# Hybrid encoder block: exponentials kept in SBUF, eight score buffers, reciprocals by four, other PSUM banks, and w's high parts on GpSimd

## The chip, the cores and the metric

The kernel runs on one core of a Trainium2 chip. Its metric is the device time of one launch in microseconds. PE is TensorE's matrix multiplier, PEld its weight loads, DVE is VectorE, ACT is ScalarE, POOL is GpSimd and SP is SyncE, which here only issues DMAs.

## The reference

One mixer layer on x of 1024 tokens by 1024 features: one projection into eight column sections, two kinds of attention, a gate, an output projection, and a LayerNorm with a scaled residual. All in float32.

```python
h = jnp.einsum('bsd,de->bse', x, w_in[layer])
q_a, k_a, v_a, z_a, q_b, k_b, v_b, z_b = jnp.split(h, SPLIT_POINTS, axis=-1)
y_a = neighborhood_attention(q_a, k_a, v_a, rel_pos_bias[layer])    # 8 heads of 64; 16 x 64 grid, window 8 x 16
qb = rotary(q_b, positions)                                         # 8 query heads
kb = rotary(k_b, positions)                                         # 2 key and value heads
y_b = windowed_gqa_with_sink(qb, kb, v_b, sink_logits[layer])       # |i - j| <= 128, softmax with one sink logit more
mixed = jnp.concatenate([y_a * jax.nn.silu(z_a), y_b * jax.nn.silu(z_b)], axis=-1)
y = jnp.einsum('bse,ed->bsd', mixed, w_out[layer])
x = layer_norm(DEEPNORM_ALPHA * x + y, ln_gain[layer], ln_bias[layer])
```

## The kernel before

Every float32 factor of a matmul is split into a high and a low 16-bit part, and a product is three matmuls: high by high, high by low and low by high (`xf`, `wh`, `wl`, `split`, `m`, `wo` are such parts). There are three phases: a prologue (values, scales, the first six projections), the stage of the attention units with the other 15 projections filled in between, and the output projection with the LayerNorm (`final`).

The order of the first two phases is written out by hand: each engine runs its instructions in the order in which the program issues them, and waits at each for what it needs. The stage is a loop over steps `i`, one attention unit a step, 128 units: first group b (64 units, the grouped-query heads with the sink), then group a (64 units, the neighbourhood heads). A unit is 128 queries of one head against 256 or 384 keys. Four units make a quad. Names and lines:

- `stage_load` (L766) runs seven steps ahead of a unit and loads the bias of a head in group a.
- `stage_qk` (L778) multiplies queries and keys on PE into a PSUM bank `ps_s` (L800). Of these there are four, used in turn. Then one DVE instruction (L807) adds mask or bias, writes the negated scores to an SBUF buffer `sn` (four, in turn) and leaves the row minimum in `nm`. In group b the column after the scores holds the negated sink, which DVE copies there (L804) for the first four units of a head pair.
- `stage_exp` (L813) lets ACT write the exponentials back into the PSUM bank of the scores (L822), with their row sums in `sm`.
- `stage_ri` (L825) makes the reciprocals of two row sums on DVE (L827) and scales them by 2 to the 14 (L828), every second step, ahead of that step's `stage_qk`.
- `stage_tr` (L832), `LTT` = 2 steps after the scores, reads the exponentials in the PSUM bank twice: ACT writes the normalised high part (L838) and DVE the low part (L839) to a `split` tile, of which there are `NSPLIT` = 6. A DMA from SP transposes it into a `tr` tile, of which there are `BH` = 9. L839 is the last to read the score bank.
- `stage_pv` (L849) multiplies a quad's transposed tiles with the values on PE (L867), `LPP` + 3 = 9 steps after the quad's first scores. Two quads share one PSUM bank `ps_t`, of which there are two. `stage_gate` (L870) multiplies the sum with the gate on DVE (L878, L881).
- `project` (L362) makes one section of 128 columns in 48 groups of matmuls (L382) into the banks `ps_pj`, of which there are two. `new_group` (L357) sees to it that the evacuation of the group two before has been issued. `w_split` (L185) splits a half of a section's weights: ACT writes the high part (L193), POOL scales the raw weights (L198) and subtracts (L199).
- `FILL_AT` says at which steps the groups of each projection, and then of the first output matmuls (L1002), are put between the units on PE. The last five entries are those of the output matmuls.
- Work that no unit waits for stands in a queue for each engine (`enq`, L149), is taken from there a little at each step (`pop`, L161), and is issued at once where it is needed (`need`, L169).

## Time and profile before

| | us |
|---|---|
| median of 3 runs (472.32 to 1610.4) | 475.13 |
| the profiled execution | 474.88 |
| its span, first to last instruction | 473.2 |

A profile comes from one execution. A row of a group names the line, engine and operation, then output and inputs by the program's names with partitions x elements and type and the count; then the busy time in us and the mean of one in ns; then the idle time of the engine just before these instructions, in us, and what ended most of it. A row of the timeline has start and length in us, and in brackets the idle time before it and its releaser. Times of PE are modelled at their ends, so a busy PE need not be PE at its peak; idle time of PE is idle.

The slices of the page, 40 of 11.8 us each in tenths of busy time, show the three phases: prologue to slice 10, the units from slice 11 to 33, the output after that.

```
PE   8999999999988998998989998789897889999995
DVE  5969868169878899888987888788988875549955
ACT  5849689774689877776786877678786874602411
POOL 0200244748468359575332664455552304104731
```

### The profile page before, as it was taken

The numbers are of one execution on the slowest core, as the hardware profiler recorded it, in microseconds if no ns is written. First come the engines' busy times: TensorE is split into PE (matmuls) and PEld (weight loads), VectorE is DVE, ScalarE is ACT, GpSimd is POOL, SyncE is SP. The second block draws the span as 40 slices with busy tenths as digits, with TensorE's granted clock in tenths as the row PEclk, the third lists the DMA queues.
The fourth block names the chain that finished last, engine by engine and source line by source line (L and its number), as shares of the span: only waits on it lengthen the run. The fifth ranks groups of instructions, "written<-read, shape, count | busy, mean of one in ns | idle before, by whom it ended". The sixth has DMA issues, their size and how long they took to land. (4 is left out here: it accounts for less than half of the span.)

```text
span 473.2 us, 11261 instructions
## 1 busy us (share of the span) xinstructions
PE 440.9 (93%) x4214; PEld 283.9 (60%) x4214; DVE 372.0 (79%) x904; ACT 319.4 (68%) x700; POOL 208.5 (44%) x219
## 2 busy tenths in 40 slices
PE   8999999999988998998989998789897889999995
PEld 7997744444555766665766765556565565444444
DVE  5969868169878899888987888788988875549955
ACT  5849689774689877776786877678786874602411
POOL 0200244748468359575332664455552304104731
PEclk9999999999999999998999999999998999999999
DMA  8911779941298896685798486486587868501721
GB/s 275 388 57 47 245 219 317 308 157 43 79 194 164 171 175 131 109 144 111 142 142 121 82 158 124 74 139 125 107 161 141 145 113 273 202 0 66 224 89 68
DMA packets 123991, 71.33 MB, mean 151 GB/s; under 512 B 96800, under 2 KB 105888, under 8 KB 123936
## 3 DMA queue, kind: packets, MB, share of 16 engines
q1 hardware_dynamic: 123792, 70.48, 63.3%
q8 instruction: 33, 0.54, 0.5%
q14 instruction: 22, 0.18, 0.1%
q10 hardware_dynamic: 144, 0.13, 0.1%
HBM read 41.23 MB, written 6.29 MB: 100 GB/s over the span
## 5 line engine op out<-in xcount | busy, mean ns | idle before, releaser
L382 PE MATMUL ps_pj<-xf,wh 128*64 128x512 f16 (+1 forms) x1152 | 210.9, 381 | 0.0
L382 PE MATMUL ps_pj<-xf,wl 128*64 128x512 f16 (+1 forms) x576 | 134.3, 381 | 0.0
L382 PEld LDWEIGHTS <-wh 128*64 128x64 f16 (+1 forms) x1152 | 82.4, 108 | 47.1 <-issue 0.6
L839 DVE SCALAR_TENSOR_TENSOR split<-ps_s,ri,split 128x384 f16<-128x384 f32 (+1 forms) x128 | 74.6, 583 | 24.6 <-ACT split L838 22.2
L838 ACT ACTIVATE split<-ps_s,ri 128x384 f16<-128x384 f32 (+1 forms) x128 | 69.7, 545 | 31.8 <-issue 12.6
L822 ACT ACTIVATE ps_s<-sn,nm 128x385 f32<-128x385 f32 (+3 forms) x128 | 70.9, 554 | 20.3 <-DVE nm L807 19.2
L800 PE MATMUL ps_s<-ks,qs 128*64 128x384 f16 (+1 forms) x512 | 63.3, 318 | 21.9 <-DVE split L839 19.4
L1002 PEld LDWEIGHTS <-m 128*128 128x128 f16 (+1 forms) x492 | 42.6, 101 | 39.9 <-issue 1.4
L800 PEld LDWEIGHTS <-qs 128*64 128x64 f16 x512 | 33.8, 110 | 52.1 <-issue 31.2
L382 PEld LDWEIGHTS <-wl 128*64 128x64 f16 (+1 forms) x576 | 42.4, 109 | 28.1 <-issue 0.4
L198 POOL TENSOR_SCALAR wr<-wr,wsc 128x512 f32<-128x512 f32 x26 | 20.5, 789 | 74.3 <-ACT wh L193 63.5
L807 DVE CUSTOM_DVE_ANT_0 sn<-ps_s,bm,nsk 128x384 f32<-128x384 f32 (+1 forms) x64 | 40.7, 636 | 1.3 <-PE ps_s L800 1.0
L1002 PE MATMUL ps_s<-wo,m 128*128 128x512 f16 (+2 forms) x228 | 40.5, 368 | 0.4 <-DVE split L839 0.4
L807 DVE CUSTOM_DVE_ANT_0 sn<-ps_s,bias,sg 128x384 f32<-128x384 f32 (+1 forms) x64 | 37.0, 578 | 2.5 <-PE ps_s L800 1.0
L199 POOL TENSOR_TENSOR wl<-wr,wh 128x512 f16<-128x512 f32 x26 | 32.7, 1256 | 2.2
L299 POOL COPY ks<-ks 64x512 f16<-64x512 f16 x40 | 26.1, 660 | 8.5 <-ACT ks L251 3.9
L198 POOL TENSOR_SCALAR ws<-ws,wsc 128x512 f32<-128x512 f32 x16 | 11.1, 692 | 39.3 <-ACT wh L193 29.4
L828 DVE TENSOR_SCALAR ri<-ri 128x2 f32<-128x2 f32 x64 | 25.8, 403 | 2.2
L1057 ACT ACTIVATE sd<-mv,eps 128x1 f32<-128x1 f32 x8 | 2.4, 294 | 36.3 <-DVE mv L1055 34.9
L1101 POOL TENSOR_TENSOR xr<-xr,gb 128x512 f32<-128x512 f32 x7 | 9.8, 1396 | 38.4 <-ACT xr L1098 38.4
L1002 PE MATMUL ps_pj<-wo,m 128*128 128x512 f16 (+2 forms) x168 | 26.5, 333 | 0.0
L822 ACT ACTIVATION_READ_ACCUMULATOR ps_s<-sn,nm 128x1 f32 x128 | 24.2, 189 | 0.0
(184 smaller groups left out, 788.8 us busy)
## 6 DMA issues: line engine op xcount, KB each, us to landing
ws<-in_wt SPq DMA_DIRECT2D x15, 512.0 KB, 5.5
wr<-in_wt SPq DMA_DIRECT2D x26, 256.0 KB, 3.4
wor<-in_wo SPq DMA_DIRECT2D x22, 256.0 KB, 3.4
xr<-in_x SPq DMA_DIRECT2D x8, 512.0 KB, 9.4
out<-xr SPq DMA_DIRECT2D x15, 256.0 KB, 2.0
bias<-in_bias SPq DMA_DIRECT2D x8, 448.0 KB, 4.6
wvraw<-in_wv SPq DMA_DIRECT2D x9, 320.0 KB, 5.8
xraw<-in_xT SPq DMA_DIRECT2D x11, 256.0 KB, 5.1
```

What stands on the lines that cost most here:

```text
L198: nc.gpsimd.tensor_scalar(raw, raw, scale, 1.0, op0=ALU.mult, op1=ALU.mult)
L199: nc.gpsimd.tensor_sub(l, raw, h)
L299: nc.gpsimd.tensor_copy(place(t, o, half, col), place(t, a, half, col))
L382: nc.tensor.matmul(ps[c], a[:, k % 4, c], mv, start=(k == 0 and i == 0), stop=(k == KT - 1 and i == 2))
L800: nc.tensor.matmul(ps[c, :n], q[:, c], sl[i], start=(i == 0), stop=(i == 1))
L807: nc.vector.tensor_tensor_reduce(sn[:, :n], ps[:, :n], bias_t, sg[:, c:c + 1], init, op0=ALU.add, op1=ALU.min, accum_out=nm)
L822: nc.scalar.activation(pt[:, :m], sn[:, :m], AF.Exp, bias=nm, scale=-1.0, accum_out=sm[:, k % 2:k % 2 + 1])
L828: nc.vector.tensor_scalar_mul(ri, ri, PSCALE)
L838: nc.scalar.activation(hl[:, :m, 0, :], src, AF.Copy, scale=ri)
L839: nc.vector.scalar_tensor_tensor(hl[:, :m, 1, :], src, ri, hl[:, :m, 0, :], op0=ALU.mult, op1=ALU.subtract)
L1002: nc.tensor.matmul(ps[d, cs], lh[:, 128 * t + d.start:128 * t + d.stop], rh[:, cs], start=(e == EO[0] and i == 0), stop=(e == EO[-1] and i ...
L1101: nc.gpsimd.tensor_mul(xr[:, h1], xr[:, h1], gb[:, h1])
```

## The change

Nothing that is computed changes. The exponentials go into the score buffer in SBUF, one column to the left of the scores, so that the sink's column stays as it is. There are eight such buffers, and POOL writes the sinks into them seven steps ahead. The reciprocals are made for four units at a time, behind `stage_qk`, and the scaling becomes an instruction with two tensor inputs (its maximum with the unscaled value changes nothing). Splitting comes five steps after the scores, the values nine. There are five `split` tiles and eight `tr` tiles. Of the eight PSUM banks four stay for scores, one is left for values and three are for projections. For the projections of the unit stage POOL writes the high parts of w, too. In the prologue and in `final` the banks are named anew, and the last entries of `FILL_AT` move.

```diff
@@ -25,15 +25,15 @@
 PSCALE = 2.0 ** 14
 MSCALE = 2.0 ** -44
 QSCALE = 2.0 ** -15
-LTT, LPP, BH, ND, NA, NX, F1 = 2, 6, 9, 1, 1, 6, 0.2
-NSPLIT, NP = 6, 2
+LTT, LPP, BH, ND, NA, NX, F1 = 5, 9, 8, 1, 1, 6, 0.2
+NSPLIT, NSN, NP = 5, 8, 2
 ORDER = ["zb0", "z0", "zb1", "kb", "qb0", "z1", "qb1", "zb2", "qb2", "k0", "qb3", "zb3", "q0", "z2", "k1",
          "q1", "k2", "q2", "k3", "q3", "z3"]
 NPRO = 6
 NS = 21 - NPRO
 NR = 8
 FILL = ORDER[NPRO:]
-FILL_AT = [0, 8, 17, 25, 33, 41, 49, 57, 64.5, 71.5, 78, 85.5, 93, 101, 109, 121, 123.5, 126, 128, 131, 136]
+FILL_AT = [0, 8, 17, 25, 33, 41, 49, 57, 64.5, 71.5, 78, 85.5, 93, 101, 109, 121, 124, 127, 130, 133, 138]
 ZTAG = {"z3": "zv", "zb3": "zc", "z2": "zs", "zb1": "zd", "zb2": "ze"}
 KO = (2, 3, 4, 5, 6, 7, 0, 1)
 X1_AT = ((0,), (1,), (2,), (3, 4), (5,), (6, 7), (), ())
@@ -67,7 +67,7 @@
     ps1 = ctx.enter_context(tc.tile_pool(name="ps1", bufs=1, space=PS))
 
     def bank(tag):
-        bufs = {"pj": 2, "s": 4, "t": 2}[tag]
+        bufs = {"pj": 3, "s": 4, "t": 1}[tag]
         return (ps1 if bufs == 1 else ps2).tile([128, 512], F32, tag=tag, name=f"ps_{tag}", bufs=bufs)
 
     vd = dram.tile([4, GW, ROWS, 256], F16, name="vd")
@@ -198,11 +198,25 @@
             nc.gpsimd.tensor_scalar(raw, raw, scale, 1.0, op0=ALU.mult, op1=ALU.mult)
             nc.gpsimd.tensor_sub(l, raw, h)
 
+        def hi_pool():
+            h = wp.tile([128, 4, 128], F16, tag="wh", name=f"wh{m}", bufs=4)
+            l = wp.tile([128, 4, 128], F16, tag="wl", name=f"wl{m}", bufs=4)
+            parts[m] = (h, l)
+            nc.gpsimd.tensor_scalar(raws[m], raws[m], scale, 1.0, op0=ALU.mult, op1=ALU.mult)
+            nc.gpsimd.tensor_copy(h, raws[m])
+
+        def lo_pool():
+            nc.gpsimd.tensor_sub(parts[m][1], raws.pop(m), parts[m][0])
+
         g = min(m // 2, NPRO)
         scale = wsc[:, g:g + 1]
 
-        o = enq("act", hi, load_ops.get(("w", m)), prio=0.5)
-        o = enq("pool", lo, o, prio=0.5)
+        if g < NPRO:
+            o = enq("act", hi, load_ops.get(("w", m)), prio=0.5)
+            o = enq("pool", lo, o, prio=0.5)
+        else:
+            o = enq("pool", hi_pool, load_ops.get(("w", m)), prio=0.5)
+            o = enq("pool", lo_pool, o, prio=0.5)
         w_ops[m] = o
         if m + 5 < NL:
             load_ops["w", m + 5] = enq("sp", lambda: w_load(m + 5), o)
@@ -355,8 +369,8 @@
     groups = []
 
     def new_group():
-        if len(groups) >= 2:
-            need(*groups[-2])
+        if len(groups) >= 3:
+            need(*groups[-3])
         return bank("pj")
 
     def project(name):
@@ -567,7 +581,7 @@
         def v_max(t):
             nc.vector.tensor_reduce(vm[:, t:t + 1], v32[t], axis=AXX, op=ALU.max, apply_absolute_value=True)
 
-        tags = ("pj", "pj", "s", "s", "t", "t", "s", "s")
+        tags = ("pj", "pj", "s", "s", "t", "pj", "s", "s")
         banks = [bank(t) for t in tags]
         ordered.enter_context(tc.manual_schedule())
         first_tiles()
@@ -751,7 +765,7 @@
 
     units = unit_list()
     split = [ap.tile([128, 3, 2, 128], F16, name=f"split{i}", bufs=1) for i in range(NSPLIT)]
-    sns = [ap.tile([128, 388], F32, name=f"sn{i}", bufs=1) for i in range(4)]
+    sns = [ap.tile([128, 388], F32, name=f"sn{i}", bufs=1) for i in range(NSN)]
     for t in split:
         nc.gpsimd.memset(t, 0.0)
     LD = 7
@@ -765,6 +779,9 @@
 
     def stage_load(u, i):
         g, p, j, t = u
+        if g == "b" and t < NSN // 2:
+            h = 2 * p + j
+            nc.gpsimd.tensor_copy(sns[units.index(u) % NSN][:, 385:386], nsk[:, h:h + 1])
         if g == "a" and t == 0:
             bulk["last"] = clock["step"] + 1
             bt = big_ap([128, BWIN[3]], F32, "bias")
@@ -798,43 +815,38 @@
         for i in range(2):
             for c in HALVES:
                 nc.tensor.matmul(ps[c, :n], q[:, c], sl[i], start=(i == 0), stop=(i == 1))
-        s0 = sns[units.index(u) % 4]
-        sn = s0[:, 384 - n:]
-        if g == "b" and t < 2:
-            nc.vector.tensor_copy(s0[:, 384:385], nsk[:, h:h + 1])
+        sn = sns[units.index(u) % NSN][:, 385 - n:385]
         nm = ap.tile([128, 1], F32, tag="nm", name="nm", bufs=6)
         c = min(p, 1) if g == "b" else 2
-        nc.vector.tensor_tensor_reduce(sn[:, :n], ps[:, :n], bias_t, sg[:, c:c + 1], init,
+        nc.vector.tensor_tensor_reduce(sn, ps[:, :n], bias_t, sg[:, c:c + 1], init,
                                        op0=ALU.add, op1=ALU.min, accum_out=nm)
-        st[u, "sn"] = sn
-        st[u, "ps"] = ps
         st[u, "nm"] = nm
 
     def stage_exp(u):
-        n, _c = geom(u)
+        n, _m = geom(u)
         m = n + 1 if u[0] == "b" else n
-        sn, nm = st.pop((u, "sn")), st.pop((u, "nm"))
-        pt = st.pop((u, "ps"))
+        nm = st.pop((u, "nm"))
+        s0 = sns[units.index(u) % NSN]
         k = units.index(u) % 4
-        if k % 2 == 0:
-            st["sm"] = ap.tile([128, 2], F32, tag="sm", name="sm", bufs=4)
-        sm = st["sm"]
-        nc.scalar.activation(pt[:, :m], sn[:, :m], AF.Exp, bias=nm, scale=-1.0, accum_out=sm[:, k % 2:k % 2 + 1])
-        st[u, "p"] = pt
+        if k == 0:
+            st["sm"] = ap.tile([128, 4], F32, tag="sm", name="sm", bufs=4)
+        nc.scalar.activation(s0[:, 384 - n:384 - n + m], s0[:, 385 - n:385 - n + m], AF.Exp, bias=nm, scale=-1.0,
+                             accum_out=st["sm"][:, k:k + 1])
+        st[u, "p"] = s0[:, 384 - n:384]
 
     def stage_ri(i):
-        ri = ap.tile([128, 2], F32, tag="ri", name="ri", bufs=4)
+        ri = ap.tile([128, 4], F32, tag="ri", name="ri", bufs=4)
         nc.vector.reciprocal(ri, st["sm"])
-        nc.vector.tensor_scalar_mul(ri, ri, PSCALE)
-        for k in range(2):
-            st[units[i - 2 + k], "ri"] = ri[:, k:k + 1]
+        nc.vector.scalar_tensor_tensor(ri, ri, PSCALE, ri, op0=ALU.mult, op1=ALU.max)
+        for k in range(4):
+            st[units[i - 4 + k], "ri"] = ri[:, k:k + 1]
 
     def stage_tr(u):
         n, m = geom(u)
         ri = st.pop((u, "ri"))
         pt = st.pop((u, "p"))
         hl = split[units.index(u) % NSPLIT]
-        src = pt[:, :n].rearrange("p (k c) -> p k c", c=128)
+        src = pt.rearrange("p (k c) -> p k c", c=128)
         nc.scalar.activation(hl[:, :m, 0, :], src, AF.Copy, scale=ri)
         nc.vector.scalar_tensor_tensor(hl[:, :m, 1, :], src, ri, hl[:, :m, 0, :],
                                        op0=ALU.mult, op1=ALU.subtract)
@@ -1114,7 +1126,7 @@
                     normed[0] += 1
 
         halves, normed = {}, [0]
-        for t, tag in ((0, "t"), (1, "t"), (2, "s")):
+        for t, tag in ((0, "t"), (1, "s"), (2, "pj")):
             obank[t, 1] = bank(tag)
             list(out_mms(t, 1, obank[t, 1], EO[:4]))
         for e in EO[4:]:
@@ -1122,7 +1134,7 @@
                 list(out_mms(t, a, obank[t, a], [e]))
                 if e == EO[-1]:
                     finish(t, a, obank[t, a])
-        tags = iter(("pj", "t", "pj", "t", "s", "s", "s", "s"))
+        tags = iter(("pj", "t", "pj", "s", "pj", "s", "s"))
         for t, a in ((3, 1), (4, 1), (5, 0), (5, 1), (6, 0), (6, 1)):
             ps = bank(next(tags))
             list(out_mms(t, a, ps, EO))
@@ -1181,8 +1193,6 @@
             m_queue(4 + M_AT.index(i))
         if bulk["last"] != i or (queues["sp"] and i - queues["sp"][0].born > 2):
             pop("sp", 1 if i < 118 else 3)
-        if i % 2 == 0 and 2 <= i <= NU:
-            stage_ri(i)
         if i < NU:
             u = units[i]
             if u[0] == "b" and u[3] in (0, 4):
@@ -1190,6 +1200,8 @@
             if u[0] == "a" and u[3] == 0:
                 need(*stk_ops[u[1], u[2], 0], *stk_ops[u[1], u[2], 1])
             stage_qk(u)
+        if i % 4 == 0 and 4 <= i <= NU:
+            stage_ri(i)
         q, m = divmod(i - LP - 3, 4)
         if i >= Q30 + 2:
             q, m = (NU // 4 - 2, i - Q30 - 2) if i < Q30 + 4 else divmod(i - LP - 3, 4)
```

## The prediction

> **What bounds the kernel now.** I read the page first (engines, slices), then a table of two stretches, then the waits, then one stretch of the timeline.
>
> ```profile
> span 473.2 us, 11261 instructions
> PE 440.9 (93%) x4214; PEld 283.9 (60%) x4214; DVE 372.0 (79%) x904; ACT 319.4 (68%) x700; POOL 208.5 (44%) x219
> ```
>
> The one timed execution behind this page took 474.88 us: 1.7 us around the span of 473.2. That is 0.25 us under the median of the runs shown, so I make the sum against 474.9.
>
> The change touches the attention units, which run from about 125 to 389 us. The table has group b (130 to 250) and group a (250 to 390); its columns are busy us of PE, PEld, DVE, ACT and POOL, then the granted clock.
>
> ```profile
> 130.00:250.00 120.00, 109.37 (x1378) 75.98 (x1376) 104.69 (x292) 95.01 (x232) 70.91 (x71) 0.99 0.83 150
> 250.00:390.00 140.00, 125.73 (x1607) 86.07 (x1605) 116.47 (x304) 105.96 (x257) 63.05 (x75) 0.99 0.68 123
> sum 260.00, PE 235.11 PEld 162.05 DVE 221.16 ACT 200.96 POOL 133.96; mean PE 117.55 PEld 81.02 DVE 110.58 ACT 100.48 POOL 66.98
> ```
>
> PE is idle for 260.0 - 235.1 = 24.9 us here, DVE for 38.8. What they wait for (total us, times, longest):
>
> ```profile
> DVE split L839 <- ACT split L838: 22.2, 56, 1.5
> PE ps_s L800 <- DVE split L839: 19.4, 29, 2.4
> DVE ri L827 <- ACT ps_s L822: 6.3, 21, 0.8
> ACT split L838 <- ACT wh L193: 4.5, 6, 1.0
> ```
>
> Almost all of PE's idle time stands ahead of the score matmuls (L800), and it ends with DVE's low-part instruction (L839), the last reader of a PSUM score bank:
>
> ```profile
> 204.44 0.62 DVE L839 SCALAR_TENSOR_TENSOR split<-ps_s,ri,split 128x384 f16<-128x384 f32 x1
> 205.11 0.52 PE L800 MATMUL ps_s<-ks,qs 128*64 128x384 f16 x4 [0.28 <-DVE split L839]
> ```
>
> The loop is: scores(i) need the bank of unit i-4, whose low part is only issued at step i-2, behind ACT's high part, behind the reciprocal. No engine is full; PE and DVE lock each other at about 90% and 85%.
>
> **The change part by part.** The durations:
>
> ```profile
> L839 DVE SCALAR_TENSOR_TENSOR split<-ps_s,ri,split 128x384 f16<-128x384 f32 (+1 forms) x128 | 74.6, 583 | 24.6 <-ACT split L838 22.2
> L807 DVE CUSTOM_DVE_ANT_0 sn<-ps_s,bm,nsk 128x384 f32<-128x384 f32 (+1 forms) x64 | 40.7, 636 | 1.3 <-PE ps_s L800 1.0
> L382 PE MATMUL ps_pj<-xf,wh 128*64 128x512 f16 (+1 forms) x1152 | 210.9, 381 | 0.0
> L828 DVE TENSOR_SCALAR ri<-ri 128x2 f32<-128x2 f32 x64 | 25.8, 403 | 2.2
> L827 DVE RECIPROCAL ri<-sm 128x2 f32<-128x2 f32 x64 | 10.3, 162 | 6.9 <-ACT ps_s L822 6.3
> L804 DVE COPY sn<-nsk 128x1 f32<-128x1 f32 x16 | 2.3, 146 | 0.0
> L193 ACT ACTIVATE wh<-wr,wsc 128x512 f16<-128x512 f32 x26 | 18.5, 712 | 0.1
> L193 ACT ACTIVATE wh<-ws,wsc 128x512 f16<-128x512 f32 x16 | 11.3, 708 | 0.0
> L198 POOL TENSOR_SCALAR wr<-wr,wsc 128x512 f32<-128x512 f32 x26 | 20.5, 789 | 74.3 <-ACT wh L193 63.5 <-PE ps_s L800 10.3
> L199 POOL TENSOR_TENSOR wl<-wr,wh 128x512 f16<-128x512 f32 x26 | 32.7, 1256 | 2.2
> L299 POOL COPY ks<-ks 64x512 f16<-64x512 f16 x40 | 26.1, 660 | 8.5 <-ACT ks L251 3.9 <-DVE ks L257 1.8 <-DVE ks L259 1.2
> L315 ACT ACTIVATE rp_raw<-ps_pj 128x512 f32<-128x512 f32 x10 | 5.9, 590 | 6.3 <-PE ps_pj L382 6.3
> L908 ACT CAST m<-z 128x512 f16<-128x512 f32 x8 | 4.5, 611 | 0.0
> L878 DVE SCALAR_TENSOR_TENSOR z<-ps_t,zc,z 128x512 f32<-128x512 f32 x8 | 5.9, 742 | 0.0
> ```
>
> *Exponentials in SBUF, pipeline longer by three steps.* The score bank is then free after the reduction (L807) of its own step, four steps before scores(i+4) need it, where it now comes free two steps before. The 19.4 us wait has no cause left. What is late next is whichever engine has most work, so the sum goes by DVE's and PE's work.
>
> *The price of it: L839 reads two SBUF tensors.* Today one of its inputs is in PSUM, and it is never held up: at most 620 ns. Two other DVE instructions that read SBUF alone, the scaling of the reciprocals (L828) and the same form in the split of W_out (L967), are:
>
> ```profile
> L839 DVE SCALAR_TENSOR_TENSOR split<-ps_s,ri,split x128: 475/617/620, 127.2 to 389.0; 128x384 f16<-128x384 f32 x96, 128x256 f16<-128x256 f32 x32
> L828 DVE TENSOR_SCALAR ri<-ri x64: 169/190/1171, 126.4 to 387.6; 128x2 f32<-128x2 f32 x64
> L967 DVE SCALAR_TENSOR_TENSOR wo<-wor,wos,wo x7: 739/742/1644, 282.5 to 404.6; 128x512 f16<-128x512 f32 x7
> 202.44 1.27 POOL L318 TENSOR_TENSOR rp_sw<-rp_sw,sin 128x512 f32<-128x512 f32 x1
> 202.83 0.91 DVE L828 TENSOR_SCALAR ri<-ri 128x2 f32<-128x2 f32 x1
> 433.01 1.26 POOL L1102 TENSOR_TENSOR xr<-xr,bb 128x512 f32<-128x512 f32 x1
> 433.09 1.20 DVE L1064 SCALAR_TENSOR_TENSOR nmr<-mv,rstd 128x1 f32<-128x1 f32 x1
> ```
>
> (Three lines of minimum/median/maximum ns, then two pairs of the timeline.) The DVE instruction of 2 elements begins under a POOL instruction and ends with it, 203.74 and 203.71; so does L1064, a scalar_tensor_tensor of one element whose two inputs are in SBUF. So the changed L839, and the new scaling of the reciprocals too, wait out whatever POOL is running. Bounds for this wait w, per instruction: 0, and 1.0 us (1171 - 169 ns, the longest shown). I take the mean that L828 pays now, 403 - 169 = 234 ns, because it is an instruction of the same steps under the same POOL load.
>
> [...]
>
> Without the wait, SBUF and PSUM sources cost the same by the rows: 742 ns for 512 elements in L878 (PSUM) and in L967's median (SBUF). So 0. [...]
>
> *Reciprocals by four.* 64 pairs leave (25.8 + 10.3 = 36.1 us), 32 come: 32 x (0.162 + 0.17 + w). Twice the width (4 elements for 2) costs nothing I can read. Moved behind the reduction, the reciprocal meets exponentials that are older by the 0.64 us of L807, so of the 6.3 us wait I keep 0 to 3.
>
> *Sinks on POOL.* 16 DVE copies (2.3 us) leave; 32 POOL copies come, for which no row stands: between 0 and the 0.66 us of POOL's copy L299, I take 0.15 as on DVE. Each waits for the exponential of the step before on ACT, with POOL's later work queued behind; the cover is seven steps until the value is used.
>
> DVE's work in the stage, in us: 221.2 - 36.1 - 2.3 + 32 x 0.33 + (128 + 32) x w = 193.4 + 160 w. At w = 0.234 it is 230.8, and PE's is 235.1.
>
> *High parts of w on POOL.* Thirty of the 42 L193 instructions leave ACT: 30 x 0.71 = 21.3 us, some of what L838 stands behind today. ACT's read of SBUF for PSUM costs back (0.611 - 0.590) x 128 = 2.7. POOL gets 30 copies, bounded by 0.66 (L299, also a copy) and 1.26 (L199, two inputs); I take 0.66: 19.8 us. POOL's 134.0 us become some 159 of 260. The chain of one part is then 0.79 + 0.66 + 1.26 = 2.7 us on one engine, for 0.71 + 0.79 + 1.26 = 2.8 on two, hidden by the eight steps of a projection; if POOL falls behind, PE's projections stand still, which is a part of the second rival.
>
> *Banks and rings.* The third projection bank saves nothing: L382 shows no idle time before it. The single value bank is read one step after the values are summed (0.74 us, L878) and written again three steps later, at 260/128 = 2.0 us each: hidden. Uncovered, it would cost up to 0.74 for each of 16 pairs of quads. With eight transposed tiles, the transpose of unit 4q+8 (step 4q+13) follows the value matmuls that free its tile (step 4q+12), which stand ahead of that step's scores on PE; SP doesn't wait for them, nor the loads queued behind on SP. Five split tiles leave five steps, 10 us, for a transpose:
>
> ```profile
> tr<-split SPq DMA_TRANSPOSE x128, 3.1
> 385.75 2.78 PE ps_s L1002 x24
> 463.28 2.69 PE ps_pj L1002 x48
> ```
>
> *The end.* From 385.75 to 466 us the chain that ended last is PE alone. Three more steps drain: 0 to 3 x 2.0 = 6 us. The output matmuls spread over those steps fill them, so I take 1.
>
> **Sum.** PE and DVE both have 231 to 235 us of work, so neither reaches the floor of 235. DVE's remaining waits for L838 shrink as ACT loses a tenth of its load and the high part no longer waits on the reciprocal just made. I take PE's idle time from 24.9 to 14: 11 us saved, 1 lost at the end. 474.9 - 11 + 1 = **465 us**; from 456 (idle 5) to 473 (idle 21, end 2) in this case.
>
> **The rivals.**
> *PE-bound.* POOL instructions held up by L839 start as it ends and run while DVE does the reduction, which reads PSUM, and are done before the next one: w = 0.1, DVE 209. PE idles some 3 us: 474.9 - 22 + 0 = 453. For it: w is a POOL matter only in part of the steps (L828's median is 190 ns). Against it: POOL gets busier.
> [...] w grows with POOL's load. In group b POOL has 70.9 of 120 us now, plus about 16 copies (10.6) and 32 sinks (4.8), and 64 L839 at 0.58 are 37: 123 of 120 us that exclude each other, if durations count in full. At w = 0.42 DVE has 193.4 + 67 = 260.6 us; with 12 us of waits left the stage is 273 and the time 488. With the same 12 us of waits and the 1 at the end it is slower than before from w = 0.34 on (193.4 + 54.4 + 13 = 260.8), and by over 2% from 0.39. For it: POOL's two-input instructions last 1.26 us, so a collision at a random moment costs 0.63. Against it: at L828's moments the mean is 0.234. [...]
> *The stall only moves.* PE now runs ahead and waits at the value matmuls for transposes instead: the slack between split and values is four steps as before, so a late DVE shows there. The time stays, 475, from 470 to 480.
>
> **Chances.** Forecast 0.42, PE-bound 0.20, port 0.26, moved 0.12. Two per cent is 9.5 us, about what a measurement of this kernel can tell from no change: faster is under 465.6. The forecast lies on that edge: 0.22 faster, 0.20 within. All of PE-bound is faster; of the port case 0.23 is slower and 0.03 within; of the moved one 0.11 within and 0.01 slower. Faster 0.42, within 0.34, slower 0.24. The range runs from 452 to 488, which leaves out the half of the port case above and a little of PE-bound below; the forecast's own is 456 to 473.
>
> **What would show it.** Right: no wait of L800 for the split; the DVE split's mean at 0.75 to 0.85 us with a maximum over 1.5; its minimum still 0.48; DVE near 231 us in the stage; the scaling at 32 instructions with the same spread. Wrong: the split stays at 0.58 to 0.65 (then 453), or goes over 1.0 with POOL full (then 488); value matmuls that wait for transposes for over 10 us; projections that wait for POOL's parts of w; PE idle for over 5 us after the last scores.

## The result, and the profile after

The changed kernel takes 471.14 us (median of 20 runs, 468.31 to 474.91) against 474.0 us for the kernel before (median of 20, of which one, 1610.4, lies far off the rest): a ratio of 0.994, with a 95% interval from 0.9919 to 0.9961. So it is a little faster, by some 0.6% where 2% had been forecast. The profiled execution of the changed kernel was its fastest, 468.31 us; a typical run has some 3 us more than the page shows.

The page, busy time by engine:

```profile
span 466.5 us, 11346 instructions
PE 438.2 (94%) x4214; PEld 282.1 (60%) x4214; DVE 371.8 (80%) x824; ACT 304.4 (65%) x670; POOL 253.5 (54%) x280
```

PE sat idle for 466.5 - 438.2 = 28.3 us of the span, where it was 473.2 - 440.9 = 32.3. So of the 6.7 us between the two spans 4.0 are idle time, and 2.7 are PE's own busy time for the same 4214 matmuls. Now the same two stretches of the unit stage as in the prediction (busy us of PE, PEld, DVE, ACT, POOL; granted clock):

```profile
130.00:250.00 120.00, 108.63 (x1376) 73.75 (x1374) 107.27 (x247) 87.32 (x217) 92.21 (x107) 1.00 0.75 146
250.00:390.00 140.00, 130.77 (x1656) 89.57 (x1656) 113.33 (x275) 103.37 (x248) 78.94 (x87) 0.98 0.75 139
sum 260.00, PE 239.41 PEld 163.31 DVE 220.60 ACT 190.69 POOL 171.16; mean PE 119.70 PEld 81.66 DVE 110.30 ACT 95.34 POOL 85.58
```

PE is idle for 20.6 us here, before 24.9; the forecast was 14. DVE's load is what it was, 220.6 for 221.2. ACT has lost 10 us, and POOL has gained 37. The waits, of the whole span, tell where the idle time went (us, times, longest):

```profile
ACT sn L833 <- DVE nm L821: 30.0, 37, 2.1
...
DVE split L851 <- ACT split L850: 21.5, 35, 2.4
...
PE ps_t L879 <- DMA tr<-split: 15.0, 14, 2.8
...
ACT sn L833 <- DVE ri L839: 11.1, 14, 1.6
...
PE ps_s L817 <- DVE qs L271: 3.7, 2, 2.5
...
PE ps_t L879 <- DVE z L890: 2.8, 3, 2.3
```

The line numbers have moved: L833 is the exponential, L850 and L851 are the high and low parts, L817 and L879 the score and value matmuls. The score matmuls' 19.4 us behind the low part are gone, as forecast. In their place PE waits 15.0 us at the value matmuls for transposed tiles. And behind that stands a wait that didn't move at all: DVE's low part waits 21.5 us for ACT's high part (22.2 before), while ACT's exponential, the instruction ahead of a high part, waits 30.0 + 11.1 us for DVE. These are the groups (busy us, mean ns; idle time ahead and what ended it):

```profile
L851 DVE SCALAR_TENSOR_TENSOR split<-sn,ri,split 128x384 f16<-128x384 f32 (+1 forms) x128 | 95.1, 743 | 22.2 <-ACT split L850 21.5
...
L833 ACT ACTIVATE sn<-sn,nm 128x385 f32<-128x385 f32 (+3 forms) x128 | 74.7, 583 | 42.2 <-DVE nm L821 30.0 <-DVE ri L839 11.1
...
L850 ACT ACTIVATE split<-sn,ri 128x384 f16<-128x384 f32 (+1 forms) x128 | 73.9, 578 | 4.2 <-DVE ri L840 2.0 <-DMA tr<-split 1.5
...
L840 DVE SCALAR_TENSOR_TENSOR ri<-ri 128x4 f32<-128x4 f32 x32 | 12.3, 386 | 1.1
...
L839 DVE RECIPROCAL ri<-sm 128x4 f32<-128x4 f32 x32 | 5.4, 170 | 0.0
```

DVE's account for the stage closes with them. The reciprocals and their scaling went from 36.1 to 12.3 + 5.4 = 17.7 us, the sinks' 2.3 left, and the low parts went from 74.6 to 95.1: -18.4 - 2.3 + 20.5 = -0.2. What the reciprocals by four saved, the low parts lost again. ACT's two instructions of a step had these rows in the kernel before:

```profile
L822 ACT ACTIVATE ps_s<-sn,nm 128x385 f32<-128x385 f32 (+3 forms) x128 | 70.9, 554 | 20.3 <-DVE nm L807 19.2
L838 ACT ACTIVATE split<-ps_s,ri 128x384 f16<-128x384 f32 (+1 forms) x128 | 69.7, 545 | 31.8 <-issue 12.6 <-ACT ps_s L822 8.7 <-ACT wh L193 4.5
```

Both have become longer, by 3.8 and 4.2 us in all. The idle time ahead of the exponential grew from 20.3 to 42.2 us, and that ahead of the high part fell from 31.8 to 4.2: in sum from 52.1 to 46.4.

The minimum, median and maximum of DVE's low part say how it lost its 20.5 us:

```profile
L851 DVE SCALAR_TENSOR_TENSOR split<-sn,ri,split x128: 472/619/1607, 131.3 to 381.5; 128x384 f16<-128x384 f32 x96, 128x256 f16<-128x256 f32 x32
```

Minimum and median are those of before (475 and 617, out of PSUM); only the tail is new. Two of the long ones and what POOL ran beside them, from the timeline (start, length):

```profile
174.25 1.61 DVE L851 SCALAR_TENSOR_TENSOR split<-sn,ri,split 128x384 f16<-128x384 f32 x1
174.28 1.16 POOL L273 TENSOR_TENSOR qs<-rp_raw,qs 64x512 f16<-64x512 f32 x1
...
204.13 1.27 POOL L333 TENSOR_TENSOR rp_raw<-rp_raw,rp_sw 128x512 f32<-128x512 f32 x1
204.23 1.19 DVE L840 SCALAR_TENSOR_TENSOR ri<-ri 128x4 f32<-128x4 f32 x1
```

The low part took 0.99 us more than its median beside a POOL instruction of 1.16; the scaling, of four elements, ended with POOL's. Over all 128 low parts the time lost is (95.1 - 74.6) / 128 = 0.16 us each. It isn't spread over them: in the timeline 46 low parts take over 0.05 us more than the undisturbed 0.62 (0.48 for 256 columns), 20.5 us together. Of these, 43 end 0.40 to 0.42 us after a POOL instruction (0.27 to 0.29 us for 256 columns); for the other three the timeline shows POOL's instructions only in groups.

How DVE and ACT hold each other up is seen in one stretch of the timeline (in brackets the idle time ahead, and its releaser):

```profile
306.99 0.61 DVE L851 SCALAR_TENSOR_TENSOR split<-sn,ri,split 128x384 f16<-128x384 f32 x1
307.16 0.61 ACT L833 ACTIVATE sn<-sn,nm 128x384 f32<-128x384 f32 x1 [1.80 <-DVE nm L821]
...
308.35 0.59 ACT L265 ACTIVATE qs<-ps_pj 64x512 f16<-64x512 f32 x1 [0.48 <-DVE qs L271]
...
308.96 0.61 ACT L850 ACTIVATE split<-sn,ri 128x384 f16<-128x384 f32 x1
...
309.61 0.86 DVE L851 SCALAR_TENSOR_TENSOR split<-sn,ri,split 128x384 f16<-128x384 f32 x1 [0.64 <-ACT split L850]
```

ACT stands for 1.80 us until DVE has the row minimum. It then does its list, an exponential, an evacuation that again waits for DVE, and only then the high part; and DVE, which issues the low part in the same step, stands until that high part is done. Neither is full (ACT 73% of the stretch, DVE 85%), and each waits for the other once a step.

### The profile page after: what moved, and what is told of

It is laid out like the page before. It is cut to its first block, busy times and chain, and to the rows that moved or that the text cites. A ratio compares the mean times of both kernels' runs of the same rounds, so it can differ in the third digit from the quotient of the medians.

```text
span 466.5 us, 11346 instructions
## 1 busy us (share of the span) xinstructions
PE 438.2 (94%) x4214; PEld 282.1 (60%) x4214; DVE 371.8 (80%) x824; ACT 304.4 (65%) x670; POOL 253.5 (54%) x280
## 4 chain that ended last, share of the span: by engine, by line
PE 53%; DVE 21%; issue 7%; ACT 6%; POOL 6%; DMA 4%; SPq 2%; DVEq 0%; POOLq 0%; ACTq 0%
PE ps_pj L396 20%; DVE split L851 8%; PE ps_pj L1014 7%; PE ps_s L1014 7%; PE ps_s L503 6%; DVE sn L821 5%; PE ps_pj L503 5%; DMA tr<-split 4%; ACT split L850 3%; PE ps_t L1014 2%; DVE qs L271 2%; PE ps_s L817 2%; PE ps_t L879 2%; DVE ks L271 2%; PE ps_t L503 2%
## 5 line engine op out<-in xcount | busy, mean ns | idle before, releaser
L851 DVE SCALAR_TENSOR_TENSOR split<-sn,ri,split 128x384 f16<-128x384 f32 (+1 forms) x128 | 95.1, 743 | 22.2 <-ACT split L850 21.5
L833 ACT ACTIVATE sn<-sn,nm 128x385 f32<-128x385 f32 (+3 forms) x128 | 74.7, 583 | 42.2 <-DVE nm L821 30.0
L850 ACT ACTIVATE split<-sn,ri 128x384 f16<-128x384 f32 (+1 forms) x128 | 73.9, 578 | 4.2 <-DVE ri L840 2.0
L817 PE MATMUL ps_s<-ks,qs 128*64 128x384 f16 (+1 forms) x512 | 62.5, 315 | 3.8 <-DVE qs L271 3.7
L817 PEld LDWEIGHTS <-qs 128*64 128x64 f16 x512 | 33.8, 111 | 26.4 <-DVE qs L271 4.7
L198 POOL TENSOR_SCALAR wr<-wr,wsc 128x512 f32<-128x512 f32 x12 | 9.6, 800 | 53.9 <-ACT wh L193 53.8
L1014 PE MATMUL ps_pj<-wo,m 128*128 128x512 f16 (+2 forms) x216 | 38.8, 344 | 0.0
L313 POOL COPY ks<-ks 64x512 f16<-64x512 f16 x40 | 29.4, 741 | 5.8 <-DVE ks L271 2.8
L879 PE MATMUL ps_t<-tr,vb 128*64 128x128 f16 x528 | 20.4, 220 | 11.6 <-DMA tr<-split 8.6
L1113 POOL TENSOR_TENSOR xr<-xr,gb 128x512 f32<-128x512 f32 x7 | 9.8, 1398 | 32.3 <-ACT xr L1110 32.3
L879 PEld LDWEIGHTS <-vb 128*64 128x64 f16 x528 | 17.3, 110 | 15.3 <-issue 10.8
L879 PE MATMUL ps_t<-tr,va 128*64 128x128 f16 x528 | 20.3, 225 | 6.4 <-DMA tr<-split 6.4
L981 POOL TENSOR_SCALAR wor<-wor,wos 128x512 f32<-128x512 f32 x9 | 9.9, 1106 | 29.9 <-DVE wo L973 24.6
```

Source lines behind the costliest of these rows:

```text
L313: nc.gpsimd.tensor_copy(place(t, o, half, col), place(t, a, half, col))
L817: nc.tensor.matmul(ps[c, :n], q[:, c], sl[i], start=(i == 0), stop=(i == 1))
L833: nc.scalar.activation(s0[:, 384 - n:384 - n + m], s0[:, 385 - n:385 - n + m], AF.Exp, bias=nm, scale=-1.0, accum_out=st["sm"][:, k:k + 1])
L850: nc.scalar.activation(hl[:, :m, 0, :], src, AF.Copy, scale=ri)
L851: nc.vector.scalar_tensor_tensor(hl[:, :m, 1, :], src, ri, hl[:, :m, 0, :], op0=ALU.mult, op1=ALU.subtract)
L879: nc.tensor.matmul(ps[c, 128 * (t % 4):128 * (t % 4) + 128], v, trs[j][:, 2 * i + w, :], start=(i + e + w == 0), stop=(i == n - 1 and w == 1))
```

## The experiments

The theory after the result: the pace of the stage is set by this loop between DVE and ACT, which the change left as long as it was; freed score banks only let PE run ahead to the next place that hangs on the loop, the value matmuls. The rivals: the slack between splitting and values is too short; the time that DVE's instructions lose beside POOL's (20.5 us in the low parts) costs the gain; the tail of the stage costs it. Ratios are to the kernel before, run on the same chip (473.5 to 473.7 us), with 95% intervals; one per cent is 4.7 us. A profile shows one execution, which can be some us off its kernel's median.

**The tail.** The end of the stage in the changed kernel's timeline (SPq is SP's queue of DMA issues):

```profile
381.52 0.48 DVE L851 SCALAR_TENSOR_TENSOR split<-sn,ri,split 128x256 f16<-128x256 f32 x1 [0.60 <-ACT split L850]
...
382.08 1.52 SPq L933 DMA_DIRECT2D wor<-in_wo  x3
...
383.71 1.19 SPq L854 DMA_TRANSPOSE tr<-split  x1
...
384.95 0.57 SPq L933 DMA_DIRECT2D wor<-in_wo  x1
...
385.61 1.06 SPq L1161 DMA_DIRECT2D gb<-in_gain  x1
...
386.78 2.62 SPq L854 DMA_TRANSPOSE tr<-split  x2
...
391.13 1.01 PE L879 MATMUL ps_t<-tr,va 128*64 128x128 f16 x29 [2.85 <-DMA tr<-split]
```

Loads of W_out and of the gain, issued at fixed steps, stand ahead of the last transposes now that splitting is three steps later: the last low part is there by 382.0, its transpose is only issued at 388, and PE waits 2.85 us. In the kernel before all transposes were ahead of these loads:

```profile
383.00 8.69 SPq L842 DMA_TRANSPOSE tr<-split  x6
...
391.75 1.99 SPq L921 DMA_DIRECT2D wor<-in_wo  x4
```

e1_late_loads puts the loads four steps later:

```diff
-WO_LD = [16, 22, 19, 25, 36, 39, 42, 45, 48, 112, 116, 28, 130, 130, 130, 130]
+WO_LD = [16, 22, 19, 25, 36, 39, 42, 45, 48, 112, 116, 28, 134, 134, 134, 134]
-        if i == 131:
+        if i == 135:
             enq("sp", gain_load, *m_ops[4])
```

> The changed kernel with the last four loads of W_out and the load of the gain queued at steps 134 and 135 for 130 and 131, behind the last transposes. Theory (SP's queue costs the end): the last four transposes are issued within 1.5 us of their low parts (for 1.9 to 6.1 us now), PE's 2.84 us of idle time before the last value matmuls goes, the time falls by 2 to 3 us (ratio to the kernel before 0.988 for 0.994). Rival (the output phase needs those loads early): PE waits for them instead in the output phase, ratio 0.994 or more.

It took 468.75 us, ratio 0.9908 [0.9878, 0.9938]. Its tail:

```profile
388.96 0.69 PE L879 MATMUL ps_t<-tr,va 128*64 128x128 f16 x18 [1.55 <-DMA tr<-split]
389.16 1.99 SPq L933 DMA_DIRECT2D wor<-in_wo  x4
...
390.42 0.49 PE L879 MATMUL ps_t<-tr,va 128*64 128x128 f16 x11 [0.76 <-DMA tr<-split]
```

The loads now come behind, but PE still waits 1.55 + 0.76 us there. The queue order was real and its place in the trace is gone; of 2.4 us between the medians (2 to 3 had been expected) the profiles account for 0.5, and the intervals of the two kernels overlap. So this is worth some 2.4 us by the medians, of the 6 by which the time came out over the forecast, and can't be all that went wrong.

**Slack or loop.** e2_slack gives the value matmuls one more step (on top of e1; loads run six steps ahead instead of seven, so that no ring grows):

```diff
-LTT, LPP, BH, ND, NA, NX, F1 = 5, 9, 8, 1, 1, 6, 0.2
+LTT, LPP, BH, ND, NA, NX, F1 = 5, 10, 8, 1, 1, 6, 0.2
-    LD = 7
+    LD = 6
```

> As e1_late_loads, and the values one step later (LPP 10; loads ahead of a unit by 6 steps for 7, so that the buffers of the values are free in time). Theory A (the stage is paced by the handshake of DVE and ACT, and PE uses up any slack that it gets): the 15.0 us that PE waits for transposes at the value matmuls turn into PE waiting at the scores or at the values still; time within 2 us of e1_late_loads. Rival B (the latency of a transpose is what costs): those 15 us fall to under 5, and the time by 5 to 10 us (ratio 0.97 to 0.98).

e3_lag keeps that and issues the low part of a unit one step behind its high part, so that DVE never asks for a high part of the same step:

```diff
         nc.scalar.activation(hl[:, :m, 0, :], src, AF.Copy, scale=ri)
+        st[u, "lo"] = hl, src, ri, m
+
+    def stage_lo(u):
+        hl, src, ri, m = st.pop((u, "lo"))
         nc.vector.scalar_tensor_tensor(hl[:, :m, 1, :], src, ri, hl[:, :m, 0, :],
...
             stage_tr(units[i - LT])
+        if 0 <= i - LT - 1 < NU:
+            stage_lo(units[i - LT - 1])
```

> As e2_slack, and DVE's low part of a unit one step behind ACT's high part instead of directly behind it. Theory A (handshake): DVE's 21.5 us of waits for the high part fall to under 5, PE's idle time in the stage falls by 8 to 15 us and the time with it: 452 to 462 us, ratio 0.96 to 0.98. Rival C (DVE's work with its collisions with POOL, 220.6 us of the 260, paces with what it must wait for anyway): the waits move to the reduction or the reciprocal, time within 3 us of e2_slack.

e2_slack took 469.57 us, 0.9919 [0.9891, 0.9947]: nothing over e1. Its waits:

```profile
DVE split L851 <- ACT split L850: 22.5, 32, 2.4
...
PE ps_t L879 <- DVE z L890: 9.3, 5, 3.0
PE ps_t L879 <- DMA tr<-split: 8.7, 8, 3.1
```

PE's wait for transposes fell from 14.4 us in e1 to 8.7, and its wait for the single bank `ps_t` (released by L890) rose from 2.9 to 9.3: the same idle time under another name. Whether a second value bank, which the kernel before has, would have let PE use the step was not run, so the single bank stays a rival for what slack is worth. e3_lag took 459.60 us, 0.9702 [0.9670, 0.9733]:

```profile
ACT sn L833 <- DVE nm L821: 18.8, 32, 1.4
...
PE ps_t L883 <- DMA tr<-split: 14.0, 14, 1.5
...
ACT split L850 <- DMA tr<-split: 8.8, 11, 1.3
...
DVE split L855 <- ACT split L850: 4.3, 5, 1.9
```

With the lag DVE's wait for the high part falls from 22.5 to 4.3 us, ACT's for the row minimum from 34.2 (e2) to 18.8, and the time by 10 us. No work was taken away; low parts even lost a little more to POOL (97.0 us for 95.9). That is the loop, shown. Not all of the 10 us is idle time, though: PE's fell from 30.7 to 24.8 us of the span, and its busy time from 437.0 to 432.9 for the same matmuls, at a granted clock of 0.989 and then 0.996. Why the clock rose was not tried. A new wait of 8.8 us shows on ACT: with the low part a step later, the five `split` tiles come free late. e7_lag_slack, e3 with still one more step for the values (`LPP` 11, `LD` 5), asks the question of slack again without the loop:

> As e3_lag, and the values one step later still (LPP 11, unit loads five steps ahead). Theory A: with the handshake gone, what is left of PE's idle time (14.0 us at the value matmuls for transposes) is a matter of slack now: it falls to under 7 us and the time by 2 to 6 us against e3_lag (ratio 0.957 to 0.966). Rival (DVE's work of 229 us of 260 in the stage paces now, and PE only uses up the slack again, as in e2_slack): time within 1.5 us of e3_lag.

It took 459.43 us, 0.9715 [0.9687, 0.9743]: again nothing, as the rival had it and not theory A. The rival's cause, that DVE's work paces now (230 of the 260 us), was not tested. PE's waits at the value matmuls are 7.4 us for transposes and 7.4 for the bank.

**The parts of the change.** e4_hi_act is the changed kernel with w's high parts back on ACT (`if g < NPRO:` becomes `if True:`).

> The changed kernel with the high parts of w back on ACT; all else as changed. Theory C (POOL's load and its collisions with DVE cost most): POOL loses 19 us of work in the stage, the mean of the split's low part falls from 743 to under 700 ns, the time falls by 2 to 5 us (ratio 0.983 to 0.990). Theory A (handshake): ACT has 20 us more to do between its exponentials and high parts, DVE's waits for high parts grow from 21.5 to 28 us or more, the time grows by 3 to 6 us (ratio 1.000 to 1.007).

474.46 us, 1.0030 [1.0004, 1.0056]. So the high parts on POOL are worth 0.9%, and without them the rest of the change is worth nothing, or a little less. POOL has 20 us less in the stage, yet the low parts' time hardly changes:

```profile
L851 DVE SCALAR_TENSOR_TENSOR split<-sn,ri,split 128x384 f16<-128x384 f32 (+1 forms) x128 | 94.7, 740 | 26.0 <-ACT split L850 25.5
```

DVE's wait for high parts is 25.5 us here against 21.5, less than the 28 that theory A had named. These two rows compare unlike executions, the slowest of e4 (479.53 us) with the fastest of the changed kernel, so that relief of ACT buys just this wait is argued and not shown. e6_hi_pool_alone is the other way round, the kernel before with only this part:

```diff
+        def hi_pool():
...
+            nc.gpsimd.tensor_scalar(raws[m], raws[m], scale, 1.0, op0=ALU.mult, op1=ALU.mult)
+            nc.gpsimd.tensor_copy(h, raws[m])
...
+        if g < NPRO:
...
+        else:
+            o = enq("pool", hi_pool, load_ops.get(("w", m)), prio=0.5)
+            o = enq("pool", lo_pool, o, prio=0.5)
```

> The kernel before with one part of the change alone: the high parts of w for the 15 later projections on POOL. Theory A: ACT stands less often between its exponential and the next high part, DVE's waits for high parts fall from 22.2 to 15 to 19 us, ratio 0.988 to 0.995. Rival (the part is worth something only beside the others): ratio 0.998 to 1.002.

471.51 us, 0.9951 [0.9935, 0.9966]: this part alone gives what the whole change gives. DVE's wait for high parts fell from 22.2 to 19.4 us only (15 to 19 had been expected), and the score matmuls still wait 19.1 us for low parts. e5_sbuf_alone is the kernel before with only the exponentials in place in SBUF (four buffers, splitting two steps after the scores, reciprocals in pairs):

```diff
-        nc.scalar.activation(pt[:, :m], sn[:, :m], AF.Exp, ...
-        st[u, "p"] = pt
+        nc.scalar.activation(s0[:, 384 - n:384 - n + m], s0[:, 385 - n:385 - n + m], AF.Exp, ...
+        st[u, "p"] = s0[:, 384 - n:384]
```

> The kernel before with one part of the change alone: the exponentials go into the score buffer in SBUF, one column to the left (four buffers, splitting two steps after the scores, all else as before). Theory A (the loop of DVE and ACT paces the stage, the score banks only show it): PE's 19.4 us of waits at the scores go, DVE pays some 20 us of collisions in the split, the 22 us that DVE waits for high parts stay or grow; the time is the same or worse, ratio 0.995 to 1.015. Rival (the score banks were the bound): ratio 0.97 to 0.985.

491.27 us, 1.0376 [1.0349, 1.0403], slower than was expected. The row of its low parts, the sum of its two stretches, and two of its waits:

```profile
L837 DVE SCALAR_TENSOR_TENSOR split<-sn,ri,split 128x384 f16<-128x384 f32 (+1 forms) x128 | 98.1, 767 | 24.8 <-ACT split L836 21.4
```

```profile
sum 260.00, PE 227.31 PEld 152.90 DVE 228.24 ACT 195.11 POOL 141.09; mean PE 113.65 PEld 76.45 DVE 114.12 ACT 97.56 POOL 70.54
```

```profile
PE ps_t L865 <- DMA tr<-split: 24.7, 19, 3.9
DVE split L837 <- ACT split L836: 21.4, 51, 1.5
```

The score matmuls wait for no low part here, as foreseen; but DVE carries 23.5 us more in low parts with nothing taken off it, the wait for high parts stays at 21.4, and most of PE's idle time (23.2 of 32.7 us in the same two stretches, 24.7 in the whole span) is at the value matmuls. So exponentials in SBUF by themselves, the freed score bank together with its price, are a loss of 3.8%. PE's own busy time is 7.5 us of it, at a lower granted clock (0.970). e9_pairs_hi_act is e4 with the reciprocals in pairs again, and so stands between e5 and e4:

```diff
-            st["sm"] = ap.tile([128, 4], F32, tag="sm", name="sm", bufs=4)
+            st["sm"] = ap.tile([128, 2], F32, tag="sm", name="sm", bufs=4)
...
-        if i % 4 == 0 and 4 <= i <= NU:
+        if i % 2 == 0 and 2 <= i <= NU:
```

> As e4_hi_act, and the reciprocals made for two units at a time again (64 pairs of instructions for 32, at every second step behind the scores). So beside e5_sbuf_alone it shows what the longer pipeline, the eight score buffers and the banks bring, and beside e4_hi_act what four at a time bring. Theory A (DVE's work lies on the loop that paces the stage): 32 x (0.16 + 0.38) = 17 us of DVE come back, of which most shows: ratio 1.02 to 1.035, which leaves the longer pipeline 1 to 8 us of the 17.7 that e5_sbuf_alone lost. Rival (DVE's work has slack, only its waits count): ratio under 1.010.

478.21 us, 1.0104 [1.0073, 1.0135], between the two expectations. Reciprocals by four are thus worth 0.7% (e9 to e4). From e5 to e9, 2.7%, come the longer pipeline with eight buffers, the other banks, the sinks on POOL and the new place and form of the reciprocals' scaling, which weren't separated. One after the other the four steps are +3.76 - 2.72 - 0.74 - 0.90 = -0.60%; they add up by construction, and in another order each could be worth something else.

**The lag, with other parts.** e8_lag_hi_act is e3 with w's high parts on ACT, e11_before_lag is the kernel before with only the lag (`LPP` 7 to keep the distance to the values).

> As e3_lag, with the high parts of w back on ACT. Theory A: what they cost on ACT was that DVE waited behind them; one step of lag covers that, so the time stays within 2 us of e3_lag (ratio 0.967 to 0.975) where it was 4.5 us without the lag. Rival (it is ACT's load itself, or POOL's, that counts): as without the lag, 3 to 6 us slower than e3_lag, ratio 0.977 to 0.984; or faster by 2 us and more, if POOL's collisions with DVE pace now.

> The kernel before with the lag alone: DVE's low part one step behind ACT's high part, the values one step later, exponentials in PSUM still. Theory A needs the score bank freed early for the lag: here the bank of unit i-4 comes free one step before scores(i) instead of two, so DVE's waits for high parts go but PE's 19.4 us of waits at the scores grow to 30 us or more: ratio 1.00 to 1.03. Rival (the lag is what counts, wherever the exponentials are): ratio 0.97 to 0.985, as good as with SBUF, and without its collisions.

e8 took 458.52 us, 0.9680 [0.9655, 0.9705]: with the loop cut, ACT can take the high parts back at no cost. In e4 against the changed kernel it could not. That fits an ACT load that mattered only through the loop, but doesn't prove it: against e3 POOL lost 15 us of work in the stage and the low parts went from 97.0 to 92.7 us, which may hide a cost on ACT. e11 took 483.72 us, 1.0209 [1.0186, 1.0232], slower than before:

```profile
DVE sn L807 <- PE ps_s L800: 31.2, 49, 1.7
PE ps_s L800 <- DVE split L843: 23.4, 37, 1.8
...
DVE split L843 <- ACT split L838: 0.3, 1, 0.3
```

The wait for the high part is gone here too (0.3 us), but the low part still frees the score bank, now a step later: PE's wait for it rose from 19.4 to 23.4 us (30 had been expected), and DVE waits 31.2 us for scores. Each of the two edits alone, exponentials in SBUF (e5) and the lag (e11), is a loss, of 3.8% and 2.1%; with the other parts of the change beside them they gain (e8). The two without the other parts were not run. e10_lag_hi_act_slack is e8 with `LPP` 11 and `LD` 5:

> As e8_lag_hi_act, and the values one step later (LPP 11, unit loads five steps ahead), the candidate for the best version. Theory A: slack at the values gave nothing twice (e2_slack, e7_lag_slack); within 1.5 us of e8_lag_hi_act, ratio 0.965 to 0.971. Rival: with ACT and POOL both relieved by the lag PE can use it, 2 to 5 us less, ratio 0.958 to 0.964.

```profile
sum 260.00, PE 245.83 PEld 162.40 DVE 224.15 ACT 210.12 POOL 163.44; mean PE 122.91 PEld 81.20 DVE 112.08 ACT 105.06 POOL 81.72
```

456.33 us, 0.9642 [0.9609, 0.9674], the best of the versions run: 3.6% under the kernel before, though its interval overlaps that of e8, and the ratio lies between the two expectations. PE's idle time in the two stretches is 14.2 us here, about the value that the prediction had taken for the change.

**DVE's time lost to POOL.** e12_no_w_low is the changed kernel with a memset in place of POOL's subtraction, so that it leaves out the low parts of w in the fifteen projections of the stage:

```diff
-            nc.gpsimd.tensor_sub(parts[m][1], raws.pop(m), parts[m][0])
+            raws.pop(m)
+            nc.gpsimd.memset(parts[m][1], 0.0)
```

> The changed kernel with a part of POOL's work left out: the low parts of w for the 15 later projections are set to zero, which reads nothing, instead of a subtraction with two inputs; all matmuls stay. It measures what POOL's collisions with DVE's split cost. Theory A (DVE's collisions are on the loop): they fall from 20.9 us to 10 to 15, the split's mean to under 0.70 us, the time by 4 to 10 us (ratio 0.973 to 0.986). Rival (the collisions fall into DVE's waits for ACT and cost nothing): the time within 2 us of the changed kernel, ratio 0.990 to 0.998.

462.04 us, 0.9762 [0.9739, 0.9785]. The low parts' time fell by 4.9 us, from 95.1 to 90.2; the kernel became some 8 us faster (0.994 to 0.976), as theory A had it, though the low parts' mean, 705 ns, is just over the 700 that it named. POOL lost 20 us of work, as in e4, but here thirty subtractions of 1.24 us became memsets of 0.52. DVE's whole busy time fell by 7.0 us (371.8 to 364.8), where the profiled spans differ by 6.4; beside the low parts, four DVE instructions `qs<-rp_raw,qs` went from 5.1 to 3.4 us. So most of the gain may be DVE's lost time. It isn't shown to be all: POOL's instructions wait as well (in the changed kernel its subtractions took 1153 to 1587 ns), and PE's busy time fell by 2.3 us, at the same profiled clock, 0.990, of which no run shows the cause. So what DVE loses to POOL costs something, and how much of the 8 us is open.

## Why the prediction was wrong

The predicted 465 us was 1.3% under what came, and the gain some three and a half times too large (9.9 us for 2.9). That the time lies in the range is no merit of the sum: DVE had 10 us less work than forecast, and PE still stood idle for longer.

- *The score wait has no cause left*: right. No score matmul waits for a low part.
- *The low part waits out POOL*: right, with a mean of 743 ns (0.75 to 0.85 had been named), a maximum of 1607 and a minimum of 472. The wait w was taken as 0.234 us per instruction and measured 0.16 for the low parts; for the scaling, whose minimum is 161 ns, it is 386 - 161 = 225 ns. DVE's work came to 220.6 us, where 230.8 were forecast. That was too careful, and it didn't help. The low part out of PSUM never took over 620 ns in the kernel before, and in e6, with the high parts of w on POOL, its mean was still 583; the one out of SBUF took up to 1607, and of the 46 long ones 43 ended 0.40 to 0.42 us after a POOL instruction (0.27 to 0.29 for 256 columns). Of the two pairs that the prediction took the wait from only the second, L1064, has two SBUF inputs; L828 has one. The second rival, port in the chances, let w grow with POOL's load to 0.42; no run shows such a w, and with POOL at 171 us of the stage it was the 0.16 and 0.225 above.
- *SBUF and PSUM sources cost the same*: right (minimum and median 472 and 619 ns against 475 and 617).
- *PE's idle time from 24.9 to 14*: this step failed. It is 20.6 in the profile. The reason given was that "DVE's remaining waits for L838 shrink as ACT loses a tenth of its load and the high part no longer waits on the reciprocal just made". They went from 22.2 to 21.5 us. Neither half of the reason held: the high part's wait for the scaled reciprocal was only 2.2 us before and is 2.0 now, and ACT lost 5% of its load in the stage and not a tenth, in part because its two instructions of a step became longer (8.0 us in all, where the prediction had 2.7). No row stood behind the 14. The sum treated DVE and ACT as loads on two engines, each with room left. But the chain of a step, row minimum on DVE, exponential and high part on ACT, low part on DVE, runs to and fro between them in program order. ACT's exponential waits 41.1 us for DVE now, where its wait for the row minimum was 19.2; that is idle time which has moved on ACT, since ahead of the high part it fell from 31.8 to 4.2. e3 cut that chain without taking work away and got 10 us, of which 5.9 are idle time of PE; in e8 ACT took its load back at no cost. How far the granted clock, the single value bank and DVE's time lost to POOL share in the missing gain stays open.
- *The rival "the stall only moves"* is what happened, with its own sign: value matmuls wait for transposes for 15.0 us, over the 10 that were to show it. It was given 0.12 and 475 us. But too little slack alone is not the cause: a step more moved the wait to the bank (e2) and gained nothing; with the lag it gained nothing in e7 and 2 us, with intervals that overlap, in e10. PE's idle time came down to about 14 us in a kernel in which this loop is cut (e10); that this is just the value of the prediction is luck, as no row led to it.
- *The end, 1 us*: the step that drains was filled by output matmuls as argued. But the prediction looked only at transposes that wait for tiles, not at the loads issued at steps 130 and 131, which stood ahead of the last three transposes on SP; PE waited 2.85 us there.
- *POOL 159 us*: 171 came. The high part took 0.71 to 0.73 us, not 0.66, the sinks 0.27, not 0.15:

```profile
L313 POOL COPY ks<-ks 64x512 f16<-64x512 f16 x40 | 29.4, 741 | 5.8 <-DVE ks L271 2.8 <-DVE ks L273 1.2
...
L784 POOL COPY sn<-nsk 128x1 f32<-128x1 f32 x32 | 8.3, 274 | 2.5 <-ACT sn L833 2.0
...
L206 POOL CAST wh<-ws 128x512 f16<-128x512 f32 x16 | 11.3, 709 | 2.8 <-PE ps_pj L396 1.9
```

That is some 1.7 us more for 30 of the one and 8.3 - 4.8 = 3.5 for the other. The rest is POOL's old work, which takes longer now. Over the whole span POOL has 253.5 us for 208.5; of these 45.0 the new instructions are 10.2 + 11.3 + 8.3 = 29.8, and the other 15 are mostly the same instructions as before: the copies of `ks` (L299 before) went from 660 to 741 ns, the scaling of `ws` (L198 before) from 692 to 860. POOL waits out DVE, too, which the 159 left out: nine of the ten subtractions (L209) that begin under a low part end 1.01 to 1.03 us after it.
- *The single value bank is hidden*: not wholly. PE waited 2.8 us for it, in three waits of which the longest is 2.3.
- A slip in the description: the values come `LPP` + 3 = 12 steps after a quad's first scores, nine being the value of `LPP`.

## What to carry to other kernels

When two engines that aren't full each show a wait for the other, lay their instructions of one step in a row and look for a chain that goes to and fro within the step; taking 21 us of load off one of them gave 0.5 to 0.9% here, while issuing the last link a step later gave 2.2% (e2 to e3) by cutting the chain. But the later link must not hold a buffer that the next step needs (e11). A wait that is removed should be priced by what stands next on the same chain, not by the free time of the engines. And when a stage is made later, look at everything that is issued at fixed steps on the queues it now falls behind.

## What the runs showed of the hardware

- The low part at 174.25 began 0.03 us ahead of POOL's instruction and still ended 0.42 us after it, just as those that began well behind one; two more, at 197.60 and 272.94, began 0.04 us ahead and ended 0.28 and 0.41 us after. At 156.44 the same 0.04 us were enough, and POOL's instruction ended 1.02 us after the low part. So a recorded start that is earlier by this little doesn't tell which of the two waits.
- The low parts' lost time was not set by POOL's busy time alone: with POOL at 171, 151 (e4) and 141 us (e5) of the stage, the low parts took 95.1, 94.7 and 98.1 us. In e12, with the same 151 us but POOL's subtraction replaced, they took 90.2; the thirty memsets took 523 ns in the mean, where the subtractions had taken 1.24 us. With the lag the two did fall together, from 179 and 97.0 us (e3) to 164 and 92.7 (e8).
- A transpose kept SP's queue for 1.2 us in the median, by which 128 of them take 155 us:

```profile
L854 SPq DMA_TRANSPOSE tr<-split x128: 1188/1212/2406, 131.8 to 388.1; - x128
```

- The profiled granted clock did not follow PE's idle time alone: it was 0.970 in e5, where PE idles 490.6 - 448.4 = 42.2 us, and 0.994 in e11 with 482.3 - 444.7 = 37.6; 0.984 in e1 with 28.2, 0.990 in the changed kernel with 28.3, and 0.996 in e3 with 24.8. Over the runs it was 0.977 to 0.992 for the changed kernel, where 17 of the kernel before, run beside e1, have 0.987 to 0.998. In e5 it was 0.96 and 0.95 in the two stretches of the unit stage, and PE was busy 7.5 us longer than in the kernel before for the same 4214 matmuls. What sets the clock, and what it costs the changed kernel, wasn't tried.
